# First norm from the token tiles, parameters on ScalarE's queue, roots in PSUM, and products of two chunks in turn

## The chip, the core and the metric

The kernel runs on one core of a Trainium2 chip. The core has a matmul engine (TensorE, "PE" in the profile, with its weight loads as "PEld"), a vector engine (VectorE, "DVE"), a scalar engine (ScalarE, "ACT"), GpSimd ("POOL") and SyncE ("SP"), which here only issues DMAs. Each engine works through its own queue in order. Engines wait for one another through semaphores; a DMA is issued from an engine's queue and runs beside it. The metric is the device time of one execution in microseconds (us); less is better.

## The reference, cut to what matters

The reference is a float32 network of two blocks on a sequence of 1024 tokens of width 1024. The first block puts 16 learned tokens in front, so it has 1040.

```python
def rmsnorm(x, g):
    y = x * rsqrt(mean(x * x, axis=-1, keepdims=True) + 1e-6)
    return y * g

def first_block(x, meta_tokens, ...):
    h = concatenate([meta_tokens, x])             # 1040 tokens
    proj = rmsnorm(h, g_pre) @ w_in               # u, q, k, v, o, gates
    y_a = gelu(s5_ssm(u)); y_a = y_a * sigmoid(y_a @ w_glu)
    y_b = headnorm(mlstm(q, k, v, gates)) * sigmoid(o)
    merged = sigmoid(ga) * (y_a @ w_a) + sigmoid(gb) * (y_b @ w_b)
    h = h + rmsnorm(merged @ w_out, g_post)
    h = h + rmsnorm((gelu(dwconv(n(h) @ w_gate)) * (n(h) @ w_up)) @ w_down, g_ffn_post)
    return h[16:]

def second_block(x, ...):
    proj = rmsnorm(x) @ w_in_2
    # a recurrent mixer (RWKV-7): per head and token
    #   state = state * w_t + (state @ -kk_t) (kk_t a_t)^T + v_t k_t^T;  y_t = state @ r_t
    # and a dilated attention on the other half of the columns
    x = x + concatenate([y_rwkv, y_attn]) @ w_out_2
    x = x + (silu(dwconv(gate)) * val) @ w_down_2   # gate, val from rmsnorm(x)
    return rmsnorm(x)
```

## The kernel before

Activations lie transposed, 128 features on the partitions and tokens along the row, in eight tiles `xh[k]`, `xl[k]`. Every large float32 product is made of three: each operand is split into a high and a low part (`whi`, `wlo`, `xh`, `xl`; `split_to`, lines 165 to 170), and `mm3` (lines 193 to 198) adds high by high, high by low and low by high in one PSUM bank. Weights come as 128-column blocks of 512 KB through SP's queue (`dma`, line 142), are scaled by the norm's gain on POOL (`wraw`), cast to `whi` on ScalarE (line 170), and the rest `wlo` is made on DVE. The norm's factor of each token, `rs`, is multiplied in when a finished bank is taken out of PSUM. Three banks (`pm`) take large products, five (`px`) everything else in the first block.

The program is written stage by stage, but a scheduler sets the order on each engine from its own model of time; semaphores are then put in, and a tile's buffer is given out anew when its last reader is done. The DMAs issued from SP and ScalarE take their semaphores in turn from eight, DMAHW0 to DMAHW7, so that an issue can wait for the DMA that had the same semaphore before.

Four places matter here.

**The start** (`params`, lines 243 to 279, and `load_x`, lines 337 to 367). `params` loads 23 small vectors into three stacks (`pst`), each transposed on PE (L264) into `par`. `load_x` loads nine token tiles `xn` (the 16 learned tokens and eight of 128), and for each of three groups of tokens (272, 384, 384 columns) and each k it transposes them on PE into a `px` bank (L356), casts to `xh` on ScalarE (L359), subtracts to `xl` on DVE, and squares the bank on ScalarE (L159, `acc` for k = 0, then `sq`), which POOL adds into `acc`. `rstd_chunk` ends a group: the sums over features are matmuls with a column of ones (L292).

**The root** (`rstd`, lines 298 to 313, and `rsqrt_small`). From the sums in PSUM it makes mean plus epsilon, then a first guess by integer arithmetic and three Newton steps, all in small DVE operations on three tiles `rst` in SBUF. A diagonal `rdg` and a product with ones (L310) spread the result over the partitions; for the first norm ScalarE copies it to `rs` (L312). The kernel calls it for every later norm too: 16 calls (output of the mixer and its new sum in the first block, both feed-forward stages, and the output of the second mixer).

**The recurrent stage** (`rwkv`, eight units of 128 tokens, four chunks of 32 each). `rwkv_unit` prepares a unit; `rwkv_maps` (L1447 to L1475) makes for each chunk c a map `A` of 96x96 for each of eight heads: two batches of four matmuls with 32 rows (L1473, rows 32c to 32c + 31 of the operands, so `tile_position` is (32c, 0)), each batch in one bank from `map_ps` (in turn `pc` and `pm`), which DVE adds to `A`. `rwkv_chain` then steps the state through the chunks (L1501). Large products of other stages stand between these on PE.

Of the kernel before, what the change touches and what calls it, by code (L numbers as in the profile page):

```python
# [10 lines left out]
I32 = mybir.dt.int32  # L11
AF = mybir.ActivationFunctionType
ALU = mybir.AluOpType
# [4 lines left out]
P = 128  # L18
D = 1024
KD = 8  # L20
NM = 16
T1 = 1040
# [4 lines left out]
EPS = 1e-6  # L27
# [16 lines left out]
TOK = [(0, 16)] + [(16 + 128 * i, 144 + 128 * i) for i in range(8)]  # L44
# [4 lines left out]
class Build:  # L49
# [197 lines left out]
    def params(self, specs):  # L247

        nc = self.nc
        res, group, rows = {}, [], 0  # L250

        def flush():
            nonlocal group, rows
            if not group:
                return
            st = self.wp.tile([P, P], F32, tag="wraw", name=self.nm("pst"))
            if rows < P:
                nc.gpsimd.memset(st, 0.0)
            r = 0
            for _, src, n in group:  # L260
                self.dma(out=st[r:r + n, :], in_=src)
                r += n
            ps = self.q_ps([P, P])
            nc.tensor.transpose(ps, st, self.ident)  # L264
            t = self.cst([P, rows], name="par")
            nc.vector.tensor_copy(t, ps[:, :rows])
            r = 0
            for name, _, n in group:
                res[name] = t[:, r:r + n]
                r += n  # L270
            group, rows = [], 0

        for name, src, n in specs:
            if rows + n > P:
                flush()
            group.append((name, src, n))
            rows += n
        flush()
        return res

# [12 lines left out]
                                  start=start and i == 0, stop=stop and i == n - 1)  # L293

    def sums_ps(self):
        return self.q_ps([P, 4])

    def rstd(self, ps, w, n, out=None):

        nc = self.nc  # L300
        nb, bw = self.blocks(w)
        m, r, t = (self.small([P, 4], tag=f"rst{i}", bufs=2)[:bw, :nb] for i in range(3))
        self.ts(m, ps[:bw, :nb], 1.0 / n, ALU.mult, EPS, ALU.add)
        self.rsqrt_small(r, m, t)
        d = self.slot([P, 4, P], name="rdg", tag=self.rdg)[:bw, :nb, :bw]
        self.tt(d, self.ident[:bw, :bw].unsqueeze(1).to_broadcast([bw, nb, bw]), r.unsqueeze(2).to_broadcast([bw, nb, bw]),
                ALU.mult)
        res = self.q_ps([P, w])
        for i in range(nb):
            nc.tensor.matmul(res[:, i * bw:i * bw + bw], self.ones[:bw, :], d[:, i], start=True, stop=True)  # L310
        if out is not None:
            nc.scalar.copy(out, res)  # L312
        return res
# [24 lines left out]
    def load_x(self):  # L338
        nc = self.nc
        self.xh = [self.slot([P, T1], F32R, "xh", "XH") for _ in range(KD)]  # L340
        self.xl = [self.slot([P, T1], F32R, "xl", "XL") for _ in range(KD)]
        acc = self.slot([P, T1], name="acc")
        self.rs = self.slot([P, T1], name="rs", tag="R")
        nat = []
        for i, (a, b) in enumerate(TOK):
            t = self.slot([P, D], name="xn", tag="Y" if i < 8 else "U")
            src = self.I["meta_tokens"] if i == 0 else self.I["x"][0, a - NM:b - NM, :]
            self.dma(out=t[:b - a, :], in_=src)
            nat.append(t)
        for g in range(3):  # L350
            toks = TOK[3 * g:3 * g + 3]
            g0, g1 = toks[0][0], toks[-1][1]
            for k in range(KD):
                ps = self.q_ps([P, g1 - g0])
                for i, (a, b) in enumerate(toks):
                    nc.tensor.transpose(ps[:, a - g0:b - g0], nat[3 * g + i][:b - a, k * P:(k + 1) * P],  # L356
                                        self.ident[:b - a, :b - a])
                h, l = self.xh[k][:, g0:g1], self.xl[k][:, g0:g1]
                nc.scalar.copy(h, ps)  # L359
                self.tt(l, ps, h.bitcast(F32), ALU.subtract)  # L360
                if k == 0:
                    self.act(acc[:, g0:g1], ps, AF.Square)
                else:
                    sq = self.small([P, 512], tag="sq", bufs=self.nsq)[:, :g1 - g0]
                    self.act(sq, ps, AF.Square)
                    self.tt(acc[:, g0:g1], acc[:, g0:g1], sq, ALU.add, eng=nc.gpsimd)
            self.rstd_chunk(self.rs, acc, g0, g1, D)

    def spill_x(self):

# [962 lines left out]
    def removal(self, j, k):  # L1333

        nc = self.nc
        kk, sq, rn = (self.slot([P, T2], name="rm", tag="A") for _ in range(3))
        self.ts(kk, k, self.par["k_k"][:, j:j + 1], ALU.mult)
# [111 lines left out]
    def rwkv_maps(self, unit):  # L1449

        nc = self.nc
        LR, KT, R, dz, wd = unit
        for c in range(4):
            self.dma(out=self.xt[32 * c:32 * c + 32, :, 32 * c:32 * c + 32], in_=dz[c].rearrange("h s t -> s h t"))
        for k in range(2):
            ps = self.map_ps([P, 4, 96])
            for h in range(4):
                nc.tensor.matmul(ps[:, h], self.xt[:, 4 * k + h], LR[:, 4 * k + h, 0], start=True, stop=True)
            nc.scalar.copy(LR[:, 4 * k:4 * k + 4, 0], ps)
        maps = []  # L1460
        for c in range(4):
            if c % 2 == 0:
                two = self.slot([96, 2, 8, 96], name="A", tag="A")
            A = two[:, c % 2]
            r = slice(32 * c, 32 * c + 32)
            self.dma(out=A[64:], in_=KT[r])
            nc.scalar.copy(A[:64, :, :64], self.ident[:64, :64].unsqueeze(1).to_broadcast([64, 8, 64]))
            for e in range(2):
                nc.scalar.copy(A.rearrange("p (q e) t -> p e q t", e=2)[:64, e, :, 64:], R[64 * e:64 * e + 64, :, r])
            for k in range(2):  # L1470
                ps = self.map_ps([96, 4, 96])
                for h in range(4):
                    nc.tensor.matmul(ps[:, h], LR[r, 4 * k + h, 0], LR[r, 4 * k + h, 1], start=True, stop=True, tile_position=(32 * c, 0))  # L1473
                self.tt(A[:, 4 * k:4 * k + 4], A[:, 4 * k:4 * k + 4], ps, ALU.add)
            maps.append(A)  # L1475
        return maps, wd

    def map_ps(self, shape):
# [656 lines left out]
```

## Time and profile before

| what | value |
|---|---|
| median of three runs | 3275.0 us (3272.95 to 3275.8) |
| the profiled execution's own time | 3284.44 us |
| its span, first to last instruction | 3282.7 us |
| mean granted TensorE clock | 0.931 of full |
| PE busy | 3067.0 us, 93% |
| DVE, POOL, ScalarE busy | 2024.9 us (62%), 1355.5 us (41%), 1145.9 us (35%) |
| shares of the chain that ended last | PE 64%, DVE 11%, issue 4%, DMA 4%, POOL 3% |

The profile is of one execution. Rows in order of time give the start and duration in us, the engine, line, operation, result and operands, and in brackets how long the engine had been idle and what ended that. Several equal instructions in a row stand in one row with their count, and the duration is that of the whole row. [...] A group's mean is of one instruction.

### The profile page before, as it was taken

How to read it: one execution, taken by the hardware profiler on the slowest of the kernel's cores; microseconds unless marked ns; L12 is line 12 of the kernel's file. 1: busy time of each engine (PE TensorE's matmuls, PEld its weight loads, DVE VectorE, ACT ScalarE, POOL GpSimd, SP SyncE). 2: the span in 40 equal slices, each digit the busy share in tenths (PEclk: the TensorE clock that was granted, in tenths of full speed). 3: DMA queues.
4: the chain of work that ended last, by engine and by line, in shares of the span. 5: the costliest groups of instructions: out<-in, count | busy, mean ns of one | idle time of the engine just before them, and what ended most of it. 6: DMA issues, size and time to landing. Idle time of an engine off the chain costs nothing.

```text
span 3282.7 us, 52740 instructions
## 1 busy us (share of the span) xinstructions
PE 3067.0 (93%) x20636; PEld 2728.9 (83%) x20636; DVE 2024.9 (62%) x3567; ACT 1145.9 (35%) x2177; POOL 1355.5 (41%) x1311
## 2 busy tenths in 40 slices
PE   6989999989989999999999999898998799999998
PEld 5989999979879999977777777786877688887777
DVE  5565663674676666466776555548665866664666
ACT  3343423334343433411333323233444433334111
POOL 4777420023564444322432355543213655444430
PEclk8999999989789999999889978877999799999999
DMA  3332621324312222422223553543336122224321
GB/s 101 100 97 92 193 91 55 112 94 135 93 60 82 78 78 78 167 78 91 76 92 130 161 116 104 115 114 105 110 106 209 45 84 77 82 79 160 129 84 52
DMA packets 322534, 336.82 MB, mean 103 GB/s; under 512 B 60081, under 2 KB 270734, under 8 KB 322286
## 3 DMA queue, kind: packets, MB, share of 16 engines
q1 hardware_dynamic: 289646, 310.38, 30.6%
q10 hardware_dynamic: 32640, 23.08, 2.3%
q8 instruction: 162, 2.65, 0.3%
q14 instruction: 86, 0.70, 0.1%
HBM read 232.66 MB, written 96.40 MB: 100 GB/s over the span
## 4 chain that ended last, share of the span: by engine, by line
PE 64%; DVE 11%; issue 4%; DMA 4%; POOL 3%; ACT 1%; SPq 1%; ACTq 0%; DVEq 0%; POOLq 0%
PE pm L196 13%; PE pm L197 13%; PE pm L198 13%; PE px L197 5%; PE px L196 5%; PE px L198 5%; DVE dn L149 2%; PE pc L1501 1%; PE px L292 1%; PE pa L1834 1%; DVE t L149 1%; POOL Z L149 1%; POOL fs L149 1%; SPq L142 1%; PE pc L1581 1%
## 5 line engine op out<-in xcount | busy, mean ns | idle before, releaser
L196 PE MATMUL pm<-xh,whi 128*128 128x512 f32 (+5 forms) x1344 | 454.4, 338 | 19.4 <-DVE th L149 10.0
L198 PE MATMUL pm<-xh,wlo 128*128 128x512 f32 (+5 forms) x1344 | 452.6, 337 | 4.6 <-DVE wlo L149 4.6
L197 PE MATMUL pm<-xl,whi 128*128 128x512 f32 (+5 forms) x1344 | 453.5, 337 | 0.9 <-DVE xl L149 0.7
L149 DVE TENSOR_TENSOR y<-y,pm 128x512 f32<-128x512 f32 (+1 forms) x336 | 218.1, 660 | 159.5 <-PE pm L198 159.1
L196 PEld LDWEIGHTS pm<-xh,whi 128*128 128x128 f32 (+1 forms) x1344 | 262.5, 195 | 43.7 <-DVE th L149 10.8
L196 PE MATMUL pm<-dn,dn 128*128 128x512 f32 (+1 forms) x736 | 285.7, 389 | 6.9 <-DVE y L149 6.4
L197 PE MATMUL pm<-dn,dn 128*128 128x512 f32 (+1 forms) x736 | 283.0, 384 | 1.3 <-POOL dn L149 1.3
L198 PEld LDWEIGHTS pm<-xh,wlo 128*128 128x128 f32 (+1 forms) x1344 | 262.3, 195 | 25.9 <-DVE wlo L149 5.1
L198 PE MATMUL pm<-dn,dn 128*128 128x512 f32 (+1 forms) x736 | 282.6, 384 | 0.0
L197 PEld LDWEIGHTS pm<-xl,whi 128*128 128x128 f32 (+1 forms) x1344 | 262.5, 195 | 21.8 <-DVE xl L149 1.7
L149 POOL TENSOR_TENSOR dn<-hid,dn 128x1024 fp32r<-128x1024 f32 x44 | 131.7, 3013 | 251.5 <-ACT dn L1140 251.5
L197 PE MATMUL px<-t,sh 128*128 128x258 f32 (+2 forms) x684 | 219.5, 321 | 5.2 <-DVE t L149 5.2
L196 PE MATMUL px<-t,sh 128*128 128x258 f32 (+2 forms) x684 | 217.1, 318 | 0.9 <-DVE up L149 0.9
L198 PE MATMUL px<-t,sl 128*128 128x258 f32 (+2 forms) x684 | 217.1, 318 | 0.0
L149 DVE TENSOR_TENSOR wlo<-wraw,whi 128x1024 fp32r<-128x1024 f32 (+2 forms) x114 | 156.6, 1375 | 79.9 <-ACT whi L170 78.3
L196 PEld LDWEIGHTS pm<-dn,dn 128*128 128x128 f32 x736 | 138.2, 188 | 44.5 <-DVE y L149 14.4
L197 PEld LDWEIGHTS pm<-dn,dn 128*128 128x128 f32 x736 | 138.4, 188 | 30.1 <-POOL dn L149 1.7
L170 ACT CAST whi<-wraw 128x1024 fp32r<-128x1024 f32 (+2 forms) x114 | 103.3, 907 | 172.0 <-PE pm L197 141.3
L198 PEld LDWEIGHTS pm<-dn,dn 128*128 128x128 f32 x736 | 138.3, 188 | 29.8
L170 ACT CAST dn<-wd 128x1024 fp32r<-128x1024 f32 x44 | 46.1, 1047 | 291.2 <-PE pm L197 290.6
L197 PEld LDWEIGHTS px<-t,sh 128*128 128x128 f32 x684 | 131.8, 193 | 16.4 <-DVE t L149 7.5
L149 DVE TENSOR_TENSOR sl<-ss,sh 128x512 fp32r<-128x512 f32 x88 | 94.1, 1070 | 79.3 <-ACT sh L170 79.2
(602 smaller groups left out, 8846.4 us busy)
## 6 DMA issues: line engine op xcount, KB each, us to landing
wraw<-in_w_in_dram SPq DMA_DIRECT2D x61, 512.0 KB
dhid<-up SPq DMA_DIRECT2D x44, 512.0 KB
wd<-in_w_ffn_down_dram SPq DMA_DIRECT2D x44, 512.0 KB
hid<-dhid SPq DMA_DIRECT2D x44, 512.0 KB
wra<-in_w_ffn_up_dram SPq DMA_DIRECT2D x33, 512.0 KB
wrb<-in_w_ffn_up_dram SPq DMA_DIRECT2D x33, 512.0 KB
dg<-th SPq DMA_DIRECT2D x16, 514.0 KB
wraw<-in_w_out_dram SPq DMA_DIRECT2D x16, 512.0 KB
```

Of the source, the lines that this page charges most:

```text
L142: self.nc.sync.dma_start(out=out, in_=in_)
L149: (eng or self.nc.vector).tensor_tensor(out=o, in0=a, in1=b, op=op)
L170: self.nc.scalar.copy(hi, src)
L196: nc.tensor.matmul(ps, a[0], b[0], start=start, stop=False, **kw)
L197: nc.tensor.matmul(ps, a[0], b[1], start=False, stop=False, **kw)
L198: nc.tensor.matmul(ps, a[1], b[0], start=False, stop=stop, **kw)
L292: self.nc.tensor.matmul(ps[:bw, i:i + 1], src[:, i * bw:i * bw + bw], self.ones[:, 0:1], start=start and i == 0, stop=stop and i == n - 1)
L1501: nc.tensor.matmul(ps[:, h], maps[c][:, h], S[:, h], start=True, stop=True)
L1581: nc.tensor.matmul(ps, w[:, k], (yh, yl, yh)[q][:, a:b], start=i == 0, stop=i == 11)
L1834: nc.tensor.matmul(self.po[:, i - 4 * ch], pT[:, i * P - a:i * P - a + P], self.vx[j % 2][:, k].rearrange("p e v -> p (e v)")[:, 2 * e:2 * ...
```

## The change

It has four parts.

1. `load_x` squares each token tile as it lies, tokens on the partitions, as soon as it has come: one Square of 128x1024 on ScalarE, whose row sums go to a column of `ss`. The squares of the PSUM banks, POOL's additions and the sums by PE go. A new function `rstd_rows` makes the root of three columns in SBUF and spreads it over the partitions; it is written after the fourth of a group's eight blocks, and DVE copies its result to `rs`.
2. `params` issues its 23 loads from ScalarE's queue (`store`) in place of SP's.
3. `rstd` keeps mean and root in eight more columns of the bank that holds the sums. Since both operands of a product would then be in PSUM, each Newton step first copies the root to SBUF.
4. `rwkv_maps` takes two chunks at a time: their loads and copies, then matmuls of the one and the other in turn, into two banks, then both additions.

```diff
--- before.py
+++ after.py
@@ params
-                self.dma(out=st[r:r + n, :], in_=src)
+                self.store(out=st[r:r + n, :], in_=src)
@@ sums_ps, rstd
-        return self.q_ps([P, 4])
+
+        return self.q_ps([P, 12])
...
-        m, r, t = (self.small([P, 4], tag=f"rst{i}", bufs=2)[:bw, :nb] for i in range(3))
+        r, t = (self.small([P, 4], tag=f"rst{i}", bufs=2)[:bw, :nb] for i in range(2))
+        m, y = (ps[:bw, 4 * i:4 * i + nb] for i in (1, 2))
         self.ts(m, ps[:bw, :nb], 1.0 / n, ALU.mult, EPS, ALU.add)
-        self.rsqrt_small(r, m, t)
+        self.ts(y.bitcast(I32), m.bitcast(I32), -0.5, ALU.mult, 1597463007.0, ALU.add)
+        for _ in range(3):
+            nc.vector.tensor_copy(r, y)
+            self.tt(t, y, r, ALU.mult)
+            self.stt(t, t, -0.5, m, ALU.mult, ALU.mult)
+            self.stt(y, t, 1.5, y, ALU.add, ALU.mult)
+        r = y
@@ load_x
-        acc = self.slot([P, T1], name="acc")
+        junk = self.slot([P, T1], name="junk")
         self.rs = self.slot([P, T1], name="rs", tag="R")
         nat = []
+        ss, r, tmp = (self.small([P, len(TOK)], tag=f"lss{i}", bufs=1) for i in range(3))
+        nc.gpsimd.memset(ss, 1.0)
...
             nat.append(t)
+            self.act(junk[:b - a, :D], t[:b - a], AF.Square, accum_out=ss[:b - a, i:i + 1])
...
-                if k == 0:
-                    self.act(acc[:, g0:g1], ps, AF.Square)
-                else:
-                    sq = self.small([P, 512], tag="sq", bufs=self.nsq)[:, :g1 - g0]
-                    self.act(sq, ps, AF.Square)
-                    self.tt(acc[:, g0:g1], acc[:, g0:g1], sq, ALU.add, eng=nc.gpsimd)
-            self.rstd_chunk(self.rs, acc, g0, g1, D)
+                if k == 3:
+                    self.rstd_rows(self.rs[:, g0:g1], *(t[:, 3 * g:3 * g + 3] for t in (ss, r, tmp)), [b - a for a, b in toks])
+
+    def rstd_rows(self, out, m, r, t, widths):
+
+        nc = self.nc
+        n = len(widths)
+        self.ts(m, m, 1.0 / D, ALU.mult, EPS, ALU.add)
+        self.rsqrt_small(r, m, t)
+        d = self.slot([P, n, P], name="rdg")
+        self.tt(d, self.ident.unsqueeze(1).to_broadcast([P, n, P]), r.unsqueeze(2).to_broadcast([P, n, P]), ALU.mult)
+        res, o = self.q_ps([P, sum(widths)]), 0
+        for i, w in enumerate(widths):
+            nc.tensor.matmul(res[:, o:o + w], self.ones[:w, :], d[:w, i, :w], start=True, stop=True)
+            o += w
+        nc.vector.tensor_copy(out, res)
@@ rwkv_maps
-        for c in range(4):
-            if c % 2 == 0:
-                two = self.slot([96, 2, 8, 96], name="A", tag="A")
-            A = two[:, c % 2]
-            r = slice(32 * c, 32 * c + 32)
...
+        for c0 in (0, 2):
+            two = self.slot([96, 2, 8, 96], name="A", tag="A")
+            rows = [slice(32 * c, 32 * c + 32) for c in (c0, c0 + 1)]
+            for i, r in enumerate(rows):
+                A = two[:, i]
...
             for k in range(2):
-                ps = self.map_ps([96, 4, 96])
+                pss = [self.map_ps([96, 4, 96]) for _ in rows]
                 for h in range(4):
-                    nc.tensor.matmul(ps[:, h], LR[r, 4 * k + h, 0], LR[r, 4 * k + h, 1], start=True, stop=True, tile_position=(32 * c, 0))
-                self.tt(A[:, 4 * k:4 * k + 4], A[:, 4 * k:4 * k + 4], ps, ALU.add)
-            maps.append(A)
+                    for ps, r in zip(pss, rows):
+                        nc.tensor.matmul(ps[:, h], LR[r, 4 * k + h, 0], LR[r, 4 * k + h, 1], start=True, stop=True, tile_position=(r.start, 0))
+                for i, ps in enumerate(pss):
+                    self.tt(two[:, i, 4 * k:4 * k + 4], two[:, i, 4 * k:4 * k + 4], ps, ALU.add)
```

The order of instructions shows how the scheduler places this. Names carry a running number.

SP's queue before, from its second DMA on (the parameters are the `pst` rows; `...` leaves out more of the same kind):

```order
L142 DMA xn_185<-in_meta_tokens_dram 16x1024
L142 DMA xn_187<-in_x_dram 128x1024
L142 DMA pst_86<-in_g_mix_pre_dram 8x128
L142 DMA pst_86<-in_g_mix_post_dram 8x128
...
L142 DMA pst_119<-in_ffn_conv_b_dram 22x128
L142 DMA pst_119<-in_ffn_conv_w_dram 66x128
L142 DMA xn_189<-in_x_dram 128x1024
L142 DMA xn_191<-in_x_dram 128x1024
...
L142 DMA xn_201<-in_x_dram 128x1024
L142 DMA dt_504<-in_ssm_log_dt_dram 128x32
L142 DMA dt_141_645<-in_ssm_d_dram 16x32x1
L142 DMA wraw_648<-in_w_in_dram 128x8x128
```

SP's queue now, its start, with the semaphores that an issue waits for:

```order
L142 DMA xn_189<-in_meta_tokens_dram 16x1024
L142 DMA xn_192<-in_x_dram 128x1024
L142 DMA xn_195<-in_x_dram 128x1024
...
L142 DMA xn_213<-in_x_dram 128x1024 [waits DMAHW0_49]
L142 DMA lst_418<-in_ssm_lambda_re_dram 32x64 [waits DMAHW2_49]
...
L142 DMA lst_418<-in_ssm_lambda_im_dram 32x64 [waits DMAHW0_49]
L142 DMA dt_428<-in_ssm_log_dt_dram 128x32 [waits DMAHW2_49]
L142 DMA dt_111_569<-in_ssm_d_dram 16x32x1 [waits DMAHW4_49]
L142 DMA bg_5170<-in_b_gates_dram 128x8 [waits DMAHW6_49]
```

ScalarE's queue now, the last third of the parameters and what follows, with the waits:

```order
L146 DMA pst_100<-in_k_a_dram 4x128 [waits DMAHW0_49]
L146 DMA pst_100<-in_r_k_dram 4x128 [waits DMAHW1_49]
L146 DMA pst_100<-in_ln_x_w_dram 4x128 [waits DMAHW2_49]
...
L146 DMA pst_119<-in_ffn_conv_b_dram 22x128 [waits DMAHW6_49,Pool_49]
L146 DMA pst_119<-in_ffn_conv_w_dram 66x128 [waits DMAHW7_49]
L159 ACT_TABLE_LOAD
L159 ACTIVATE junk_183,lss_41_185<-xn_189 16x1024
L370 CAST xh_167<-px_53_216 128x272
```

The token tiles have moved ahead of everything on SP. All 23 parameter loads stand on ScalarE ahead of its table load, its first Square and its first CAST, and several wait for a semaphore that SP's rows above also use.

DVE at one of the 16 later roots (the sums of 128x2 in the first feed-forward stage), before:

```order
L153 TENSOR_SCALAR rst_1090_8367<-rst_1089_8366 128x2
L149 TENSOR_TENSOR rst_1091_8368<-rst_1090_8367 128x2
L156 SCALAR_TENSOR_TENSOR rst_1091_8368<-rst_1091_8368,rst_1089_8366 128x2
L156 SCALAR_TENSOR_TENSOR rst_1090_8367<-rst_1091_8368,rst_1090_8367 128x2
L149 TENSOR_TENSOR rst_1091_8368<-rst_1090_8367 128x2
L156 SCALAR_TENSOR_TENSOR rst_1091_8368<-rst_1091_8368,rst_1089_8366 128x2
L156 SCALAR_TENSOR_TENSOR rst_1090_8367<-rst_1091_8368,rst_1090_8367 128x2
```

and now (`px_1054` is the bank of the sums):

```order
L153 TENSOR_SCALAR px_1054_8243<-px_1054_8243 128x2 x2
L308 COPY rst_1057_8294<-px_1054_8243 128x2
L149 TENSOR_TENSOR rst_1058_8295<-px_1054_8243,rst_1057_8294 128x2
L156 SCALAR_TENSOR_TENSOR rst_1058_8295<-rst_1058_8295,px_1054_8243 128x2
L156 SCALAR_TENSOR_TENSOR px_1054_8243<-rst_1058_8295,px_1054_8243 128x2
L308 COPY rst_1057_8294<-px_1054_8243 128x2
L149 TENSOR_TENSOR rst_1058_8295<-px_1054_8243,rst_1057_8294 128x2
L156 SCALAR_TENSOR_TENSOR rst_1058_8295<-rst_1058_8295,px_1054_8243 128x2
L156 SCALAR_TENSOR_TENSOR px_1054_8243<-rst_1058_8295,px_1054_8243 128x2
```

Mean and root have moved into the bank, and a COPY stands at the head of each Newton step.

PE in the recurrent stage at the first products of a unit, before (`pm` and `pc` are the two banks of `map_ps`, L1501 is the state's step, L1408 the products that prepare the next unit):

```order
L1473 MATMUL pm_2537_18844<-LR_18063 96x96 x4
L1473 MATMUL pc_2538_18850<-LR_18063 96x96 x4
L1408 MATMUL pq_2561_18963<-pr_18907,pr_18906 32x32 x16
L1408 MATMUL pq_2562_18981<-pr_18907,pr_18906 32x32 x2
L1501 MATMUL pc_2606_19242<-ST_18809,A_18839 96x64 x4
L1473 MATMUL pm_2539_18860<-LR_18063 96x96 x4
L1408 MATMUL pq_2562_18981<-pr_18907,pr_18906 32x32 x3
L1501 MATMUL pc_2606_19242<-ST_18809,A_18839 96x64 x4
L1473 MATMUL pc_2540_18866<-LR_18063 96x96 x4
```

and now at such a place (the products are L1495, the step L1523):

```order
L1523 MATMUL pc_2564_19190<-ST_18757,A_18787 96x64 x4
L1495 MATMUL pm_2500_18829<-LR_18011 96x96 x2
L1495 MATMUL pc_2501_18830<-LR_18011 96x96 x2
L1495 MATMUL pm_2500_18829<-LR_18011 96x96
L1495 MATMUL pc_2501_18830<-LR_18011 96x96
L1495 MATMUL pm_2500_18829<-LR_18011 96x96
L1495 MATMUL pc_2501_18830<-LR_18011 96x96
L1435 MATMUL pq_2522_18952<-ident_66,pr_18854 128x128 x4
L1435 MATMUL pq_2523_18958<-ident_66,pr_18855 128x128 x4
```

Matmuls of two chunks now stand mixed. Over the whole stage 144 of the 256 products are followed by one of the other chunk's rows, in place of a batch of four of one chunk; the rest is still in batches, since the scheduler puts them in by readiness.

## Rows read from the trace of the kernel before

**Rows 1.** the page's totals (engine, busy us, share, instructions) and its chain by engine

```profile
PE 3067.0 (93%) x20636; PEld 2728.9 (83%) x20636; DVE 2024.9 (62%) x3567; ACT 1145.9 (35%) x2177; POOL 1355.5 (41%) x1311
...
PE 64%; DVE 11%; issue 4%; DMA 4%; POOL 3%; ACT 1%; SPq 1%; ACTq 0%; DVEq 0%; POOLq 0%
```

**Rows 2.** SP's queue in time (start us, us, what), the start

```profile
2.43 0.32 SPq L142 DMA_DIRECT2D pst<-in_g_mix_pre_dram  x1
...
10.26 0.34 SPq L142 DMA_DIRECT2D pst<-in_ffn_conv_w_dram  x1
10.65 3.30 SPq L142 DMA_DIRECT2D xn<-in_x_dram  x7
```

**Rows 3.** DMA traffic, the first 40 us in slices of 1 us

```profile
GB/s 0 0 103 340 178 8 49 9 6 6 17 96 348 385 320 336 369 426 410 418 426 276 233 290 292 151 2 0 0 0 0 0 8 0 0 0 120 325 249 318
```

**Rows 4.** ScalarE in time (start us, us, what, idle before), the start

```profile
14.79 1.54 ACT L359 CAST xh<-px 128x272 fp32r<-128x272 f32 x5 [12.70 <-PE px L356]
...
58.30 0.48 ACT L359 CAST xh<-px 128x384 fp32r<-128x384 f32 x1 [0.99 <-PE px L356]
```

**Rows 5.** PE in time, the start

```profile
35.23 0.60 PE L198 MATMUL pm<-xh,wlo 128*128 128x272 f32 x1 [4.57 <-DVE wlo L149]
...
64.40 0.83 PE L292 MATMUL px<-ones,acc 128*128 128x1 f32 x6 [1.09 <-POOL acc L149]
68.20 1.62 PE L310 MATMUL px<-rdg,ones 128*128 128x128 f32 x6 [2.97 <-DVE rdg L149]
...
72.51 0.60 PE L196 MATMUL pm<-xh,whi 128*128 128x272 f32 x1 [2.14 <-DVE ra L153]
```

**Rows 6.** busy time by stretch (stretch, us, each engine, PEclk, DMA)

```profile
60.00:75.00 15.00, 8.77 (x36) 7.74 (x35) 8.07 (x31) 4.12 (x6) 5.92 (x5) 0.61 0.16 45
75.00:90.00 15.00, 15.00 (x91) 15.00 (x91) 13.68 (x53) 2.07 (x3) 7.05 (x8) 0.91 0.87 111
```

**Rows 7.** ScalarE by form, 0:75 us (count, busy us, mean ns, idle)

```profile
L359 ACT CAST xh<-px 128x384 fp32r<-128x384 f32 x16 | 7.6, 481 | 5.9 <-PE px L356 5.9
L159 ACT ACTIVATE sq<-px 128x384 f32<-128x384 f32 x14 | 6.7, 493 | 8.0 <-DVE xl L149 4.5 <-POOL acc L149 2.2 <-DVE rst L156 1.3
L170 ACT CAST whi<-wraw 128x1024 fp32r<-128x1024 f32 x3 | 3.1, 1042 | 0.6 <-PE pm L197 0.3 <-POOL wraw L149 0.3
```

**Rows 8.** POOL by form, 0:75 us

```profile
L149 POOL TENSOR_TENSOR acc<-acc,sq 128x384 f32<-128x384 f32 x14 | 14.1, 1011 | 12.8 <-ACT sq L159 12.1
```

**Rows 9.** tile rst after 75 us (count: ns min/median/max, first, last)

```profile
L156 DVE SCALAR_TENSOR_TENSOR rst<-rst,rst x96: 149/161/1211, 797.4 to 2550.0; 128x2 f32<-128x2 f32 x48, 86x3 f32<-86x3 f32 x24, 128x4 f32<-128x4 f32 x24
...
L153 DVE TENSOR_SCALAR rst<-px x16: 144/159/163, 796.9 to 2543.7; 128x2 f32<-128x2 f32 x8, 86x3 f32<-86x3 f32 x4, 128x4 f32<-128x4 f32 x4
L153 DVE TENSOR_SCALAR rst<-rst x16: 154/169/1242, 797.0 to 2544.1; 128x2 int32<-128x2 int32 x8, 86x3 int32<-86x3 int32 x4, 128x4 int32<-128x4 int32 x4
```

**Rows 10.** DVE by form, the whole span

```profile
L156 DVE SCALAR_TENSOR_TENSOR rst<-rst,rst 86x3 f32<-86x3 f32 x24 | 9.3, 388 | 0.7
```

**Rows 11.** DVE in time, around 1615 us

```profile
1615.06 5.36 DVE L156 SCALAR_TENSOR_TENSOR y<-y,par,px 128x512 f32<-128x512 f32 x8
...
1620.74 3.41 DVE L156 SCALAR_TENSOR_TENSOR xl<-y,par,xh 128x512 fp32r<-128x512 f32 x2
```

**Rows 12.** POOL in time, the same stretch

```profile
1616.95 11.26 POOL L149 TENSOR_TENSOR y<-y,x 128x512 f32<-128x512 f32 x8
```

**Rows 13.** PE's waits, 895:912 us (us, times, longest)

```profile
PE px L310 <- DVE rdg L149: 6.0, 1, 6.0
```

**Rows 14.** PE in time, around 1963 us

```profile
1962.80 1.11 PE L1473 MATMUL pc<-LR 32*96 32x96 f32 x5
1963.56 0.47 PE L1473 MATMUL pm<-LR 32*96 32x96 f32 x1
...
1964.14 1.00 PE L1473 MATMUL pm<-LR 32*96 32x96 f32 x5
```

**Rows 15.** busy time by stretch, the recurrent stage

```profile
1950.00:2000.00 50.00, 47.98 (x512) 40.94 (x511) 22.98 (x50) 13.88 (x32) 27.94 (x88) 0.76 0.30 75
```

More of the change, by code (lines that the diff above doesn't have):

```diff
@@ L1460, in rwkv_maps @@
         maps = []
-        for c in range(4):
-            if c % 2 == 0:
-                two = self.slot([96, 2, 8, 96], name="A", tag="A")
-            A = two[:, c % 2]
-            r = slice(32 * c, 32 * c + 32)
[L1466 to L1469, printed above, removed]
+        for c0 in (0, 2):
[3 more added lines that the diff above has]
+                A = two[:, i]
+                self.dma(out=A[64:], in_=KT[r])
+                nc.scalar.copy(A[:64, :, :64], self.ident[:64, :64].unsqueeze(1).to_broadcast([64, 8, 64]))
+                for e in range(2):
+                    nc.scalar.copy(A.rearrange("p (q e) t -> p e q t", e=2)[:64, e, :, 64:], R[64 * e:64 * e + 64, :, r])
+                maps.append(A)
             for k in range(2):
-                ps = self.map_ps([96, 4, 96])
+                pss = [self.map_ps([96, 4, 96]) for _ in rows]
                 for h in range(4):
-                    nc.tensor.matmul(ps[:, h], LR[r, 4 * k + h, 0], LR[r, 4 * k + h, 1], start=True, stop=True, tile_position=(32 * c, 0))
-                self.tt(A[:, 4 * k:4 * k + 4], A[:, 4 * k:4 * k + 4], ps, ALU.add)
-            maps.append(A)
+                    for ps, r in zip(pss, rows):
+                        nc.tensor.matmul(ps[:, h], LR[r, 4 * k + h, 0], LR[r, 4 * k + h, 1], start=True, stop=True, tile_position=(r.start, 0))
+                for i, ps in enumerate(pss):
+                    self.tt(two[:, i, 4 * k:4 * k + 4], two[:, i, 4 * k:4 * k + 4], ps, ALU.add)
         return maps, wd
```

## The prediction

> **What bounds the kernel now.** I read the totals first: TensorE is busy 93% of the span and the chain that ended last lies on PE for 64% of it [rows 1]. So an edit pays where PE has nothing to do or where its own work shrinks; elsewhere it is free or wasted. Next I looked for PE's idle time near the four edits. The start is the worst stretch. SP issues the first token tile, then 23 small parameter loads from 2.43 us to 10.26 us, and only then the seven other token tiles, 10.65 to 13.95 us [rows 2]. The row of GB/s shows what follows: traffic falls to 6–49 GB/s in slices 5 to 10 and runs at 330–430 only from slice 12 to 20 [rows 3]. ScalarE's first CAST of a transposed tile starts at 14.79 us, its last one at 58.30 [rows 4]. PE waits 4.57 us for `wlo`, 1.09 for a POOL `acc`, 2.97 for the last `rdg`, and starts the second weight at 72.51 after 2.14 more [rows 5]. [...] So the first norm ends the start: squares, adds, sums, root, `rdg`, copy of `rs`, and with it the eviction that frees a `pm` bank for the second weight.
>
> **Part 1 and 2, squares as x arrives and parameters on ScalarE's queue (one sum, since they share the queue).** Removed: 24 Squares of PSUM tiles (14 of them 0.493 us [rows 7], the 7 narrower ones and 3 into `acc` alike, so at most 24 x 0.5 = 12 us of ScalarE), 21 adds on POOL (14 x 1.01 = 14.1 us [rows 8] plus seven narrower), the sums on PE, three copies of `rs` on ScalarE. Added: eight Squares of 128x1024 and a short one. None is in the trace; the nearest row is the 128x1024 CAST at 1.04 us [rows 7], the lower end the narrower form's 0.49, the upper end twice the CAST, 2.1: 8 x 1.04 = 8.3 us. So ScalarE's total hardly changes, POOL's 14 to 20 us go, and the norm no longer hangs behind the last transposed block.
>
> The x tiles are now issued first. A tile's issue takes 3.30/7 = 0.47 us [rows 2], so all eight are out by about 6 us instead of 14, and at the 330–430 GB/s of [rows 3] 4.2 MB land by about 15 us instead of 22 or more. But ScalarE now issues the 23 loads in front of its table load, its Squares and its CASTs. At (10.26 + 0.34 - 2.43)/23 = 0.355 us each [rows 2] that is 8.2 us if nothing holds them. Something does: in the new order ScalarE's load of `k_a` waits for DMAHW0, which the eighth x tile and the last `lst` load use before it, and later loads wait for the semaphores of `dt`, `d` and `bg`. Behind the waiting instruction stands all of ScalarE; PE waits for it once its five `px` banks are full, and DVE's `xl` too. I put the last x tile at 15 us, the `lst` chain two landings later, and the first CAST at 23 us against 14.79. The first weight's load waits for the buffer of a parameter stack, so its CAST comes near 29 and `wlo` near 31 (before: in time for PE at 35.23).
>
> From the first CAST to the last the new order has 8 CASTs of 272, 15 or 16 of 384 (0.48), 8 Squares (1.04) and two `whi` (1.04) on ScalarE: 3.2 + 7.7 + 8.3 + 2.1 = 21 us, so the last CAST falls near 44 instead of 58.3. After it PE needs one group of 24 matmuls; in [rows 5] the last CAST stands 14.2 us before the second weight, of which 1.09 + 2.97 + 2.14 were waits of the norm that now comes early; so 14.2 - 6.2 = 8 us, and the second weight starts at 52: a gain of 20. Bounds: not held at all, the first CAST comes at 13 and the gain is 30; held until 35, it is 8. PE is full behind this place [rows 6], so work moved forward should stay moved; the order behind it is almost the same, yet I leave 2 us to later waits on weights and tables. Value: **-18 us** (-28 to -6).
>
> **Part 3, roots in PSUM.** Each root is 11 dependent small DVE operations; the median one takes 0.16 us, some up to 1.24 [rows 9]. The 24 of the 86x3 form have a mean of 388 ns [rows 10], against 161 that is 5.4 us in four calls; for all forms in the 16 later calls I estimate 10, twice that. What they wait for is seen best on longer operations: `y<-y,par,px`, with one operand in PSUM, takes 5.36/8 = 0.67 us, and `xl<-y,par,xh`, of the same size with both in SBUF, 3.41/2 = 1.7 [rows 11]; POOL works on SBUF from 1616.95 to 1628.2 [rows 12], beside most of the first and all of the second. So DVE with two SBUF operands stalls beside POOL, and with one it does not: the roots' stalls go. In exchange each iteration gets a copy: 3 x 16 copies at about 0.195 us from start to start = 9.4 us of DVE, and the sum's bank is kept until `rdg` is made. DVE is not the bound, so only calls for which PE waits count: the longest, 6.0 us for `rdg` [rows 13], would nearly vanish, the unstalled ones get 0.6 longer. Writing PSUM from DVE in small operations has no row: below, 0.144 (the fastest read, rows 9) makes it free; above, 0.388 in place of 0.16 for eight writing operations costs 1.9 us a call, some 8 us on the four calls that PE waits for. Value: **-4 us** (-8 to +8), nearer the row that reads PSUM, the same engine and size.
>
> For the read side the trace shows no penalty: `rst<-px` has a median of 159 ns, `rst<-rst` 169 [rows 9]. [...]
>
> **Part 4, products of two chunks in turn.** A product is a 32-row matmul that leaves two records. In one stretch at the low clock, five records of one chunk start within 0.76 us (0.152 each); then, from 1963.56 to 1964.14, seven records of two chunks run mixed in 0.58 us (0.083 each), and alone again five take 1.00 [rows 14]. So two row groups do overlap, here by chance of the batches' ends. In the order 144 of the 256 products are now followed by one of the other group. 288 records x (0.152 - 0.083) = 20 us at that clock; at the full clock about half; the stage has 0.76 [rows 15], and some overlap is there already, so 12 us of PE. PE is busy 47.98 of 50 us there [rows 15], but the stage also has a serial chain through POOL, DMA and state steps, so I count about two thirds: **-8 us**. Against it: both PSUM banks are filled together, so PE no longer fills one while DVE adds the other; if that is exposed, each of 32 pairs costs an add, at most the 0.67 us of an operation in [rows 11], 21 us, most of it (I take four fifths) covered by the other matmuls in line: +4. Range -16 to +4.
>
> **Sum.** -18 - 4 - 8 = -30 us: 3284.44 (the profiled execution, span 3282.7 and 1.7 around it) becomes 3254.4. That execution lies 9.4 us above the median of the runs, 3275.0; carried over, the forecast is **3245 us**.
>
> **Rivals.**
> - *ScalarE held longer.* If the chained loads hold it until 35 us or more, part 1 and 2 give -6 and the sum is -18: 3257. For: it is in order and eight semaphores are shared. Against: x now arrives earlier. From a first CAST near 43 us the gain is gone.
> - *Products do not gain.* If the lost turn-taking of the two banks decides, part 4 is +4: -18, again 3257. For: DVE must add both banks before PE goes on; against: [rows 14].
> - *PSUM roots cost.* By the upper bound from rows, part 3 is +8 and the sum -18: 3257. For: nothing in the trace shows DVE writing PSUM this way; against: reads are as fast as ever [rows 9]. [...]
> - *Slower: the recurrent stage loses its filler.* The scheduler has reordered that stage on PE and SP. A pair of maps is ready only when the later chunk's copies and loads are; if the state steps wait for that in each of 16 pairs by a batch and an add (eight records at the 0.1 us between [rows 14]'s two rates, 0.84, plus 0.67 as above), some 24 us; with PE's idle time there (2.02 in 50 [rows 15]) growing from 4% to 14% over 380 us it is +38 us. Parts 1 to 3 give 22, so it decides from +22 on; 38 - 22 = +16: 3291. For: in-order queues and long DMA trips; against: weight matmuls stand between the products and fill.
> - *More than forecast.* ScalarE not held, products overlapping fully: -28 - 8 - 16 = -52: 3223.
>
> **How the numbers follow.** A measurement of this kernel tells 0.2% (6.5 us) from no change, so 'same' is 3268.5 to 3281.5. Chances: forecast 0.50 (own range 3236 to 3254), ScalarE held 0.17, products 0.10, roots 0.05, slower stage 0.08, more 0.10. Of the three middle rivals a fifth ends within 0.2% because two can meet (0.06), and of the forecast's own spread 0.02. Faster 0.84, same 0.09, slower 0.07. The range, leaving out the worst and best tenth: 3224 to 3268.
>
> **What would show it.** First CAST on ScalarE near 23 us, the last near 44; second weight on PE near 52 instead of 72.5; no `acc` on POOL. No small root operation above 0.2 us and PE's wait of 6.0 us for `rdg` gone. Starts of paired products at 0.08 us in the low clock, PE's idle share between 1900 and 2220 not above before's. I am wrong if the second weight starts after 65 us, if PE waits more later what it saved, or if the recurrent stage is longer than before.

## The result and the profile after

The changed kernel takes 3255.97 us (median of 4 runs, 3250.67 to 3261.54), before 3275.4: a ratio of 0.994 with a 95% interval of 0.9922 to 0.9959, so 19.4 us faster. The forecast was 3245, its range 3224 to 3268. The profiled execution took 3260.19 us (span 3258.5), 24.3 less than the profiled one of before.

The page's totals after, as in [rows 1]:

```profile
PE 3022.7 (93%) x20614; PEld 2686.7 (82%) x20614; DVE 2010.1 (62%) x3618; ACT 1138.8 (35%) x2166; POOL 1337.7 (41%) x1291
...
PE 62%; DVE 11%; POOL 5%; issue 5%; DMA 5%; ACT 2%; SPq 1%; ACTq 0%; DVEq 0%; POOLq 0%
```

PE has 44 us less to do, but only 24 us came off the span: PE's waits grew. To see where, I matched the matmuls of the two traces (same function, line and names, n-th with n-th) and took the median difference of their starts in bins of 100 us (500 stands for 500 to 600, and so on). Against before, the changed kernel is ahead by

| at (us of before) | 0–100 | 500 | 700 | 1000 | 1500 | 1800 | 2300 | 2500 | 2600 | 3200 |
|---|---|---|---|---|---|---|---|---|---|---|
| ahead (us) | 16.5 | 13.8 | 13.1 | 20.3 | 19.8 | 18.0 | 23.1 | 21.4 | 25.4 | 25.9 |

**The start.** SP's queue, then ScalarE's, in order of time ([rows 2, 4] answer to them):

```profile
1.72 7.99 SPq L142 DMA_DIRECT2D xn<-in_x_dram  x8
```

```profile
16.42 0.26 ACTq L146 DMA_DIRECT2D pst<-in_k_a_dram  x1
...
19.87 0.36 ACTq L146 DMA_DIRECT2D pst<-in_ffn_conv_w_dram  x1
20.26 1.28 ACT L159 ACT_TABLE_LOAD   x1 [20.26 <-DMA pst<-in_ln_x_b_dram]
21.56 1.06 ACT L159 ACTIVATE junk<-xn 16x1024 f32<-16x1024 f32 x1
22.52 0.18 ACT L159 ACTIVATION_READ_ACCUMULATOR junk<-xn 16x1 f32 x1
22.61 0.91 ACT L370 CAST xh<-px 128x272 fp32r<-128x272 f32 x3
...
51.67 0.48 ACT L370 CAST xh<-px 128x384 fp32r<-128x384 f32 x1 [2.61 <-PE px L367]
```

The eight token tiles go out first, but they take 7.99 us, until 9.71 (forecast about 6), where seven took 3.30. ScalarE's last parameter load goes out at 19.87 us, its first CAST follows at 22.61 (forecast 23). Each Square is followed by an ACTIVATION_READ_ACCUMULATOR (0.18 us). PE, as in [rows 5], and its load, as in [rows 6]:

```profile
32.36 0.60 PE L198 MATMUL pm<-xh,wlo 128*128 128x272 f32 x1 [1.03 <-DVE wlo L149]
...
41.52 0.94 PE L385 MATMUL px<-rdg,ones 128*128 128x128 f32 x6 [1.56 <-DVE rdg L149]
...
55.57 0.39 PE L196 MATMUL pm<-xh,whi 128*128 128x272 f32 x1
```

```profile
60.00:75.00 15.00, 15.00 (x95) 15.00 (x94) 14.29 (x33) 3.41 (x4) 8.43 (x8) 1.00 0.95 157
```

The second weight starts at 55.57 in place of 72.51 (forecast 52), and PE is full between 60 and 75 us at a granted clock of 1.00, where it was busy for 8.77 of 15 us at 0.61 [rows 6]. The last CAST came at 51.67, not at 44; it no longer mattered, as PE worked through the first weight with 1.03 and 1.56 us of waits.

**The roots.** The tile `rst`, as in [rows 9]:

```profile
L308 DVE COPY rst<-px x48: 145/158/163, 784.1 to 2522.7; 128x2 f32<-128x2 f32 x24, 86x3 f32<-86x3 f32 x12, 128x4 f32<-128x4 f32 x12
L149 DVE TENSOR_TENSOR rst<-px,rst x48: 145/159/161, 784.3 to 2522.9; 128x2 f32<-128x2 f32 x24, 86x3 f32<-86x3 f32 x12, 128x4 f32<-128x4 f32 x12
L156 DVE SCALAR_TENSOR_TENSOR rst<-rst,px x48: 142/156/159, 784.5 to 2523.1; 128x2 f32<-128x2 f32 x24, 86x3 f32<-86x3 f32 x12, 128x4 f32<-128x4 f32 x12
L156 DVE SCALAR_TENSOR_TENSOR px<-rst,px x48: 151/166/167, 784.7 to 2523.3; 128x2 f32<-128x2 f32 x24, 86x3 f32<-86x3 f32 x12, 128x4 f32<-128x4 f32 x12
```

Not one of the 192 is above 167 ns, and 79 of them overlap an instruction of POOL. Counted the same way in before, 39 of the 160 root operations with all operands in SBUF overlap one, and 23 of these took more than 200 ns; of the 121 others none did. PE's wait of 6.0 us [rows 13] is gone from its place, but in the same stretch PE now has this, and DVE does this meanwhile:

```profile
858.60 1.56 PE L318 MATMUL px<-rdg,ones 86*128 86x86 f32 x6
865.90 1.20 PE L318 MATMUL px<-rdg,ones 128*128 128x128 f32 x4 [5.75 <-DVE rdg L149]
```

```profile
859.96 0.16 DVE L308 COPY rst<-px 128x2 f32<-128x2 f32 x1
860.20 1.27 DVE L156 SCALAR_TENSOR_TENSOR y<-y,gq,px 128x258 f32<-128x258 f32 x3
861.38 0.15 DVE L149 TENSOR_TENSOR rst<-px,rst 128x2 f32<-128x2 f32 x1
861.45 2.04 DVE L156 SCALAR_TENSOR_TENSOR y<-y,gq,px 128x258 f32<-128x258 f32 x5
```

The root's operations are short, but between two of them the order puts eight `y<-y,gq,px` (1.27 us for three, 2.04 for five), and PE stands 5.75 us. Still the stretch got shorter. Before (columns as in [rows 6]):

```profile
780.00:930.00 150.00, 130.07 (x897) 126.67 (x897) 95.39 (x225) 57.80 (x140) 79.41 (x80) 0.75 0.32 95
```

After, the same work:

```profile
766.90:910.00 143.10, 121.17 (x899) 118.18 (x897) 89.19 (x249) 57.31 (x141) 77.16 (x80) 0.83 0.35 100
```

PE idles as long as before (19.9 and 21.9 us), but it is busy for 121.17 us in place of 130.07 with the same matmuls, at a granted clock of 0.83 in place of 0.75. The other kernels of the next section fall into the same two groups: in this stretch the seven with part 3 take 141.7 to 143.5 us at a clock of 0.81 to 0.83, and the five without it (before among them) 150.0 to 150.7 at 0.75 to 0.79, while PE's idle time is alike (18.5 to 21.9 and 19.9 to 23.9).

**The products.** Four consecutive records of the changed kernel at the full clock (1.00 granted from 1944 to 1946 us):

```profile
1945.09 0.24 PE L1495 MATMUL pm<-LR 32*96 32x96 f32 x1
1945.10 0.24 PE L1495 MATMUL pc<-LR 32*96 32x96 f32 x1
1945.17 0.24 PE L1495 MATMUL pm<-LR 32*96 32x96 f32 x1
1945.19 0.24 PE L1495 MATMUL pc<-LR 32*96 32x96 f32 x1
```

Two records, one of each chunk, start every 0.08 us. In before, at the same clock, neighbouring records of one chunk start 0.085 us apart (median of 260), so there one record takes the time of two here; at the low clock (0.50 granted from 1962.8 to 1965.2 us) a single one took 0.152 [rows 14]. The whole stretch from the recurrent stage through the attention behind it, before and after, between the same matmuls:

```profile
1830.00:2400.00 570.00, 518.25 (x4850) 440.62 (x4849) 336.90 (x838) 205.65 (x435) 245.47 (x579) 0.84 0.44 116
```

```profile
1812.00:2379.80 567.80, 494.53 (x4850) 416.74 (x4849) 332.24 (x838) 204.57 (x435) 239.06 (x579) 0.84 0.44 116
```

PE is busy 23.7 us less and idle 21.5 us more (51.8 and 73.3). PE's longest waits there now (us in total, times, longest):

```profile
PE pq L1435 <- DVE KT L149: 12.3, 3, 7.6
PE pc L1523 <- ACT yv L1527: 11.2, 3, 9.4
PE pm L1478 <- DMA xt<-dz: 7.7, 3, 5.2
```

The stretch gained 2.2 us.

### The profile page after: what moved, and what is told of

Read it like the earlier page. It is cut to its first block, busy times and chain, and to the rows that moved or that the text cites. A ratio compares the mean times of both kernels' runs of the same rounds, so it can differ in the third digit from the quotient of the medians.

```text
span 3258.5 us, 52664 instructions
## 1 busy us (share of the span) xinstructions
PE 3022.7 (93%) x20614; PEld 2686.7 (82%) x20614; DVE 2010.1 (62%) x3618; ACT 1138.8 (35%) x2166; POOL 1337.7 (41%) x1291
## 4 chain that ended last, share of the span: by engine, by line
PE 62%; DVE 11%; POOL 5%; issue 5%; DMA 5%; ACT 2%; SPq 1%; ACTq 0%; DVEq 0%; POOLq 0%
PE pm L196 13%; PE pm L197 13%; PE pm L198 12%; PE px L197 5%; PE px L196 5%; PE px L198 5%; DVE dn L149 2%; PE px L292 1%; POOL Z L149 1%; POOL fs L149 1%; DVE t L149 1%; PE pa L1856 1%; PE pc L1523 1%; SPq L142 1%; DVE y L149 1%
## 5 line engine op out<-in xcount | busy, mean ns | idle before, releaser
L197 PEld LDWEIGHTS pm<-xl,whi 128*128 128x128 f32 (+1 forms) x1344 | 261.4, 195 | 19.5 <-issue 0.5
L149 POOL TENSOR_TENSOR wraw<-wraw,par 128x1024 f32<-128x1024 f32 (+1 forms) x36 | 76.0, 2111 | 173.1 <-DMA wraw<-in_w_in_dram 137.5
```

Source lines behind the costliest of these rows:

```text
L149: (eng or self.nc.vector).tensor_tensor(out=o, in0=a, in1=b, op=op)
L197: nc.tensor.matmul(ps, a[0], b[1], start=False, stop=False, **kw)
```

## The experiments

Before stands in each comparison with runs of its own. "Second weight" is the start that [rows 5] show at 72.51; "ahead" is at 1000 us, by matching as above; the last three columns are of the same stretch of work as in the two rows just shown (length, and the idle and busy time of PE in it), each from the one profiled execution of that kernel.

| kernel | parts | ratio to before | second weight | ahead | length | idle | busy |
|---|---|---|---|---|---|---|---|
| before | – | 1 | 72.51 | 0 | 570.0 | 51.8 | 518.3 |
| changed | 1 2 3 4 | 0.994 (0.9922–0.9959) | 55.57 | 20.3 | 567.8 | 73.3 | 494.5 |
| e1 | 4 | 0.998 (0.9968–0.9992) | 72.31 | 1.5 | 556.6 | 64.5 | 492.1 |
| e2 | 3 | 1.0031 (1.0019–1.0043) | 73.66 | 11.0 | 591.0 | 72.5 | 518.6 |
| e3 | 2 | 1.0015 (1.0004–1.0027) | 80.83 | -5.7 | 563.1 | 54.5 | 508.7 |
| e4 | 1 | 1.0004 (0.9994–1.0014) | 50.13 | 16.7 | 587.5 | 59.3 | 528.2 |
| e5 | 1 3 4 | 0.9873 (0.9851–0.9894) | 47.63 | 30.1 | 560.5 | 67.3 | 493.2 |
| e6 | 1 2 3 | 1.0009 (0.9996–1.0021) | 57.24 | 19.5 | 590.5 | 72.1 | 518.4 |
| e7 | 1 3 4, tiles first | 0.9897 (0.9875–0.9919) | 42.91 | 29.5 | 571.6 | 68.6 | 503.0 |
| e8 | 1 2 3 4, products twice | 1.0045 (1.0031–1.0059) | 55.74 | 18.9 | 602.5 | 82.3 | 520.2 |
| e9 | 1 3 4, root later | 0.9904 (0.9891–0.9918) | 44.93 | 32.2 | 572.4 | 77.5 | 494.9 |
| e10 | 1 4 | 0.9936 (0.9921–0.995) | 49.45 | 19.2 | 569.0 | 67.4 | 501.6 |

Two theories stood against each other on each part; the texts say which numbers each wanted.

**e1, part 4 alone.** Of the diff only the hunk in `rwkv_maps`.

> Only the products of two chunks in turn (part 4); all else as before. Overlap theory: in the recurrent stage PE has about 24 us less to do (as in the profile after: 350.7 to 326.8 us) and the stage is bound by PE, so the whole gets 8 to 24 us faster, 3251 to 3267. Serial-chain theory: PE's work falls by the same 24 us, but PE then waits for the solve on POOL, its round trip by DMA and the state steps; the whole gains at most 6 us, 3269 to 3275, and PE's idle time between 1850 and 2230 us grows from about 29 us to about 50.

```profile
1831.80:2388.40 556.60, 492.06 (x4850) 415.23 (x4849) 335.57 (x838) 204.81 (x435) 242.52 (x579) 0.86 0.44 119
```

PE's work fell by 26 us, the stretch by 13, the median of the whole by 6 (3272.91 to 3279.32). Both theories hold half: the overlap is real, and PE's idle time takes half of it back (between 1850 and 2230 it grew from 29.3 to 45.5 us, near the 50 of the second theory).

**e2, part 3 alone.** Only the hunk in `sums_ps` and `rstd`.

> Only the roots in PSUM (part 3). Stall theory: no small root operation above 0.2 us any more, PE's wait of 6.0 us near 904 us gone; 4 to 9 us faster, 3266 to 3271. Cover theory: the stalls were beside other work, the copies add as much as the stalls took; within 3 us of before.

```profile
1818.70:2409.70 591.00, 518.55 (x4850) 433.60 (x4849) 336.54 (x838) 205.64 (x435) 248.09 (x579) 0.84 0.42 112
```

Slower as a whole, and yet 11 us ahead at 1000 us. All of that and more goes in the recurrent stretch, where part 3 changes nothing (no root lies between 1660 and 2520): PE is as busy as before (518.55), and idle 20.7 us more. So the expectation held for the place of the edit, and missed what came 1000 us later.

**e3, part 2 alone.** Only the hunk in `params`.

> Only the parameter loads on ScalarE's queue (part 2), the squares and sums of the first norm as before. If the earlier token tiles are what pays: second weight on PE near 58 us and 14 us faster, 3261. If the norm behind the last transposed block is what ends the start: ScalarE's first CAST near 22 us (held by the loads), 24 Squares still to do behind it, second weight at 68 to 76 us, within 4 us of before or slower.

```profile
20.37 0.96 ACT L359 CAST xh<-px 128x272 fp32r<-128x272 f32 x3
```

```profile
72.48 1.44 PE L292 MATMUL px<-ones,acc 128*128 128x1 f32 x6 [1.08 <-POOL acc L149]
76.83 1.62 PE L310 MATMUL px<-rdg,ones 128*128 128x128 f32 x6 [2.90 <-DVE rdg L149]
...
80.83 0.60 PE L196 MATMUL pm<-xh,whi 128*128 128x272 f32 x1 [2.04 <-DVE ra L153]
```

ScalarE's first CAST came at 20.37 us, the chain of `acc`, sums and `rdg` ended the start just as before, and the second weight came 8.3 us later than before (80.83, beyond the 68 to 76 expected). The queue alone costs time; the earlier tiles bring nothing while the norm ends the start.

**e4, part 1 alone.** Only the hunk in `load_x` with `rstd_rows`.

> Only the squares from the token tiles (part 1), parameters on SP ahead of seven of the tiles as before. If the norm is what ends the start: first CAST near 15 us, second weight near 57 to 60 us, 10 to 15 us faster, 3260 to 3265, so the queue is not needed. If the late tiles end it: second weight above 66 us and at most 6 us faster.

```profile
50.13 0.39 PE L196 MATMUL pm<-xh,whi 128*128 128x272 f32 x1 [1.77 <-DVE ra L153]
```

The second weight starts 22.4 us earlier, more than with parts 1 and 2 together and before the 57 to 60 expected, and 16.7 us of it are there at 1000 us. The 10 to 15 us expected of the whole did not come (1.0004): the recurrent stretch is 17.5 us longer. Part of that is this execution's own, which took 3291.03 us against a median of 3279.35: PE is busy 10 us longer there with the same matmuls.

**e5, the changed kernel without part 2.** The `store` of e3 taken back.

> The changed kernel with the parameter loads back on SP (parts 1, 3, 4). From the single runs: the start gives 16 to 18 us without the queue, the roots near 900 us give 7 to 11, so by 1500 us it is 24 to 28 us ahead of before (the changed kernel is 20 ahead there). If the queue move is what helps: less than 18 ahead there. The end depends on the recurrent stage: by its PE work alone 3245; if the stage's order falls badly as in the runs with squares or roots alone, 3262.

```profile
15.13 1.22 ACT L370 CAST xh<-px 128x272 fp32r<-128x272 f32 x4
```

```profile
31.73 0.39 PE L198 MATMUL pm<-xh,wlo 128*128 128x272 f32 x1 [1.32 <-DVE wlo L149]
...
47.63 0.39 PE L196 MATMUL pm<-xh,whi 128*128 128x272 f32 x1 [1.78 <-DVE ra L153]
```

ScalarE's first CAST comes at 15.13, the second weight at 47.63, 7.9 us before that of the changed kernel, and 30.1 us ahead stand at 1000 us. The stretch behind it falls better too (560.5). With 3241.2 us against 3281.3 it beats both kernels: ratio 0.9873.

**e6, the changed kernel without part 4.** The old loop of `rwkv_maps` put back.

> The changed kernel with the old loop of products (parts 1 to 3). By the stage's own work: 20 us ahead of before at 1500 us as the changed kernel, and it keeps that, 3258. If without the 24 us of saved PE work the stage loses as in the runs with squares or roots alone (16 to 20 us): 3272 to 3276.

```profile
1808.70:2399.20 590.50, 518.43 (x4850) 435.72 (x4849) 334.13 (x838) 205.41 (x435) 242.55 (x579) 0.84 0.42 112
```

The second case came: nothing left of 19.5 us. Against the changed kernel the stretch is 22.7 us longer, with PE's idle time alike (72.1 and 73.3): between these two the whole of part 4's saving counts.

**e7, token tiles first on SP, the parameters behind them.** `load_x` split in two (cut, with comments added):

```diff
+            B.load_tiles()          # the nine DMAs of xn, first of all
             B.par = B.params([...])  # its 23 DMAs on SP
```

> The changed kernel, but SP issues the nine token tiles first and the 23 parameter loads behind them, none on ScalarE. ScalarE is not held: first CAST at 12 to 14 us in place of 22.6, second weight on PE near 46 to 48 instead of 55.6, so 8 us ahead of the changed kernel in the first block. If the first weight's load (it waits for the parameter stacks) ends the start instead: second weight at 54 to 57, no gain.

```profile
7.71 0.65 ACT L376 CAST xh<-px 128x272 fp32r<-128x272 f32 x2
```

```profile
42.74 0.46 PE L196 MATMUL pm<-xh,whi 128*128 128x384 f32 x2
43.03 0.29 PE L197 MATMUL pm<-xl,whi 128*128 128x272 f32 x1
```

ScalarE begins at 7.71 us, even before the forecast 12. The row of two holds the second weight's first matmul, the ninth of 272 columns with `whi`: it starts at 42.91, among the last ones of the first weight and 4.7 us before e5's. The first weight is later in exchange: its load goes out at 23.28 us and its matmuls start at 32.48, in e5 at 21.87 and 29.21. Between 100 and 300 us e7 is 27 us ahead of before and e5 21, at 1000 us the two are level (29.5 and 30.1). The recurrent stretch is 11.1 us longer than e5's, and the whole 0.9897.

**e8, every product twice.**

```diff
-                    for ps, r in zip(pss, rows):
+                    for ps, r in 2 * list(zip(pss, rows)):
```

> The changed kernel with every product of the recurrent stage done twice into the same place, about 30 us more for PE there. If PE bounds the stage: 25 to 35 us slower than the changed kernel, near 3285. If the serial chain bounds it: at most 10 us slower, PE's idle time in the stage falls by 20 or more.

```profile
1811.20:2413.70 602.50, 520.16 (x5362) 443.60 (x5361) 329.72 (x838) 204.63 (x435) 237.09 (x579) 0.84 0.42 110
```

PE is busy 25.6 us more than in the changed kernel, the stretch is 34.7 us longer, and the whole 34 us by the two ratios. So the added work counts in full, and PE's idle time rises by 9.0 us where the second theory wanted it to fall by 20: that theory falls as it was put. But the maps wait for their products, so this run also lengthens the serial chain, and it does not show that PE alone bounds the stage.

**e9, as e5 with the root of the first norm written later.**

```diff
-                if k == 3:
+                if k == 7:
```

> As the run with the loads back on SP, but the first norm's root is written after the eighth block of a group and not the fourth. Nothing of the recurrent stage is touched, yet the scheduler puts a third of that stage's matmuls in another order. If the stage's time hangs on what its work is: within 4 us of that run, 0.986 to 0.989 of before. If it hangs on the order the scheduler happens on: the stage alone differs by 6 to 20 us, and PE's idle time there by as much, while its busy time stays within 5 us.

e5, then e9:

```profile
1800.90:2361.40 560.50, 493.23 (x4850) 417.02 (x4849) 333.34 (x838) 204.72 (x435) 238.73 (x579) 0.85 0.45 118
```

```profile
1797.20:2369.60 572.40, 494.88 (x4850) 417.89 (x4849) 332.46 (x838) 203.56 (x435) 243.80 (x579) 0.84 0.44 115
```

The edit lies at the start, where it is worth 2.7 us. In the recurrent stretch PE's busy time differs by 1.7 us, but its idle time by 10.2, and the stretch is 12 us longer. That is what the second theory wanted. But how much the order differs depends on how it is counted: told apart by names and shapes alone, 95.0% of PE's matmuls of the stretch stand in one common sequence in e5 and e9. In e5 and the changed kernel 98.7% do, and these two still differ by 6.0 us of idle time and 7.3 us of length. So differences more than half as large as e9's come with nearly the same order. The intervals of the two ratios (0.9851–0.9894 and 0.9891–0.9918) just touch.

**e10, as e5 without part 3.** `rstd` and `sums_ps` of before.

> As the run with the loads back on SP, but without the roots in PSUM (parts 1 and 4). If the roots are worth what their place near 900 us shows: 7 to 9 us less ahead of before at 1000 us (21 to 23 in place of 30), and 0.989 to 0.991 of before if the recurrent stage falls the same. If the stalls are covered: 28 or more ahead there.

The stretch of [rows 13] without part 3 (e10), then with it (e5):

```profile
762.10:912.70 150.60, 127.83 (x902) 124.80 (x901) 96.24 (x226) 58.03 (x143) 79.02 (x80) 0.79 0.32 95
```

```profile
758.30:900.80 142.50, 121.27 (x900) 117.58 (x899) 92.85 (x250) 58.59 (x143) 73.96 (x80) 0.83 0.34 101
```

8.1 us longer without part 3, and again at a lower clock (0.79 and 0.83, half the difference between before and the changed kernel); 19.2 ahead at 1000 us, 10.9 less than e5 where 7 to 9 were expected. The roots pay at their place. The whole is 0.9936, above the 0.989 to 0.991 expected, as the recurrent stretch fell 8.5 us longer than e5's.

## Why the prediction was right, and where not

**Parts 1 and 2.** The mechanism was right: the norm's chain ended the start, and its removal moved the second weight to 55.57, forecast 52. By 500 us 13.8 us are left of 16.9 (I had taken 2 off, it was 3). Wrong was to put both parts in one sum. e3 and e4 show part 1 worth 22.4 us at the second weight and part 2 costing 8: the hold of ScalarE, which the prediction had described (first CAST at 23 in place of 14.79), brought nothing in exchange. What the hold costs is on PE: of the 72 transposes of token tiles, 57 are done in e5 when the first weight's `wlo` product starts (31.73 us), but only 33 in the changed kernel (32.36); the others stand among that weight's matmuls, when PE has little time to spare: from there to the second weight it is busy 21.24 of 23.10 us with 129 matmuls, in e5 13.87 of 15.90 with 91. With ScalarE held the earlier tiles bring nothing (e3); with it free (e7) they are worth 4.7 us at the second weight, and nothing any more at 1000 us. The other sign that failed here is the last CAST, at 51.67 instead of 44.

**Part 3.** The stalls went as forecast. Reading PSUM did not make these operations longer: each of the four forms of `rst` shown above reads it, and they have medians of 156 to 166 ns, the longest that of the form that also writes it, against 161 for `rst<-rst,rst` [rows 9]. (The upper bound for small writes to PSUM was added up a little high: 8 x (0.388 - 0.16) is 1.8 us a call, 7 on four calls, not 8.) The size was off, 7 us near 900 us instead of 4, and the step that failed is "PE's wait of 6.0 us would nearly vanish": a wait of 5.75 us stands elsewhere in the same stretch, and PE's idle time there is unchanged. What fell is PE's busy time, by 8.9 us at a granted clock of 0.83 instead of 0.75. Why the clock was granted higher no run here isolates; that the stretch is shorter with part 3 is seen in all seven kernels that have it, and in none of the five without it.

**Part 4.** The overlap was there: 23.7 us less work for PE in the stretch, more than the 12 I took. Those rest on "at the full clock about half", the author's estimate, which no row shows: there a record of one chunk takes 0.085 us and one of two in turn 0.04, so 0.045 us are saved in place of 0.069, about two thirds. The net was 2.2 us instead of 8 in the changed kernel, 13 alone (e1), 22.7 against e6. The step that failed is "two thirds of it count": against e6 nearly all of PE's saving counted, against before a tenth, because the stretch's idle time is no constant of the kernel. It was 51.8 us before and 54 to 82 in eleven other kernels, five of which leave the stage's code untouched (e2, e3, e4, e6 and, against e5, e9). Each of these figures is of one execution, and how far two executions of one kernel differ there was not measured; for e2 the times bear it out, since it is 11 us ahead at 1000 us and its five runs are still 10 us slower than before in the median. Before has the least idle time of all, so each of these edits starts with a loss there. The rival "the recurrent stage loses its filler" thus came true in half, with 21.5 us of idle time in place of 38, and not for the pairs alone: e2 and e6 have as much (72.5 and 72.1) without them. Whether the pairs add some is open (64.5 us and more in the kernels with them, 54.5 to 72.5 in the changed ones without). The 4% of idle time that the rival started from were read from one stretch of 50 us [rows 15]; from 1900 to 2220 it was 24.2 of 320 us before and is 42.8 of 314.8 now, so the sign "PE's idle share between 1900 and 2220 not above before's" failed.

**The sum.** -14 at the start, +1 up to 700, -7 near 900 us, +2 around 1650, where four of the later roots lie, -2 in the recurrent stretch with the attention, -5 around 2550, where the last four roots lie: some -25, and -24.3 between the two profiled executions, against -30 forecast; -19.4 between the medians, whose runs of one kernel spread over 11 us. That the sum came out near the forecast is in part luck: the start gave 5 us less than its term and part 4 six less, and the place near 900 us gave 3 more and the one around 2550 five that no term had. The last five are not all of part 3: between 2440 and 2640 the kernels with it gain 2.5 to 5.9 us on before, those without lose 0.9 to gain 3.1. The 2 lost around 1650 are not its doing either, as e1 and e4, without it, lose 3 to 4 there.

What stays open: what makes the recurrent stretch's idle time 52 or 77 us. The scheduler's order is the likeliest cause, since the stage's own code stays as it is under an edit elsewhere, but this is argued and not shown: e9 fits it, while the changed kernel and e5, nearly alike in order, differ by 6.0 us. The moment at which the stage's work arrives is the rival, and no run here holds the one fixed and moves the other.

## What to carry to other kernels

An edit that is bundled with another is worth trying alone and left out: here the bundle gained 0.6%, and without one of its four parts 1.3%. When a scheduler orders the program, look at the trace stage by stage against the same matmuls, since an edit that gains in its own place can lose as much in a stage that it never touched; a total of zero (e4, e6) says little about the edit. Before moving transfers to another queue, ask what in-order work stands behind them there and whether anyone waits for what arrives earlier.

## What the runs showed of the hardware

In the changed kernel an accumulating Square of 128x1024 took 1.05 us, the one of 16x1024 as long (1.06), and each was followed by an ACTIVATION_READ_ACCUMULATOR of 0.18 us. Small DVE operations that read PSUM took 142 to 167 ns here, beside POOL (79 of 192) or not; with all operands in SBUF they took up to 1.24 us [rows 9], and more than 0.2 us only beside POOL. 32-row matmuls on two row groups started in pairs every 0.08 us at a granted clock of 1.00, where records of one group followed at 0.085; at 0.50, where records of one group followed at 0.152 us, records of two groups followed at 0.083 [rows 14].
